# One queue for x and the first weights of a four-branch decoder trunk, with its scheduler's constants fitted anew

## The chip, the cores and the metric

The kernel runs on one core of a Trainium2 chip. Its time is device microseconds of one execution, and the number compared is the median of several runs. TensorE (PE in the profile, PEld for its weight loads) multiplies matrices, VectorE (DVE) and ScalarE (ACT) work on elements, GpSimd (POOL) fills constants and moves a few small tiles, SyncE (SP) issues most loads. ACT and POOL can issue loads too; "SPq", "ACTq" and "POOLq" are the issuing sides of these engines.

## The reference

One layer of a decoder trunk on x of 256 tokens by 1024 channels, float32. A row norm, one projection to 4104 columns, four branches side by side of 256 channels each, a projection back, a second row norm, and the residual:

```python
h = rmsnorm(x, pre_norm_g[l])
proj = jnp.einsum('btd,dc->btc', h, w_in[l])
p_gdn, p_hgrn, p_moba, p_diff = jnp.split(proj, splits, axis=-1)
y = jnp.concatenate([gdn_branch(...), hgrn2_branch(...), moba_branch(...), diff_branch(...)], axis=-1)
y = jnp.einsum('btc,cd->btd', y, w_out[l])
x = x + rmsnorm(y, post_norm_g[l])
```

"gdn" is a gated delta rule in chunks of 64 tokens with a short convolution ahead of it, "hgrn" a gated linear recurrence, "moba" a causal softmax attention (with 256 tokens only one block), "diff" the difference of two softmax attentions. Each has four heads and a SiLU gate.

## The kernel before

**Operands.** Every large product is done in a reduced float32 format (fp32r) as three products of high and low parts: hi·hi + lo·hi + hi·lo. A weight pair (two blocks of 128 rows of one column group, 512 or 520 columns wide) is loaded into a buffer `raw` (six of them), and `split` makes `whi` (a rounding copy, on ACT) and `wlo` (a subtraction, on DVE) from it, four buffers each. x comes transposed (`pxt`, 35 columns of small parameters and then eight blocks of 128 channels by 256 tokens). For each block, `hT_hi` is a scaled copy on ACT, `hT_lo` a subtraction on DVE. The row norm of x is not applied there: it is worked out from `xs`, x in rows, and multiplied in after the projections (`rs`, and `rrow`, its copy along the free axis).

**Column groups.** `w_in` is stored in eight groups: gkq, gv (gdn), hqf, hiz (hgrn), mqk, mvz (moba), dqk, dvz (diff). `piece` loads and splits a pair when a projection first asks for it. gkq comes first and consists of four pairs: row blocks 0 and 1, 2 and 3, 4 and 5, 6 and 7. For each row block, four matmul groups of three products write to two banks of `pj`. The first pair is treated apart: its two blocks are loaded and split one after the other, and block 0 is rounded on DVE. The other pairs are loaded and split whole.

**Loads of the start.** The tile `px` (traced as h_kd, whose memory it shares) takes the 35 parameters and block 0 of x, and the tiles `xr` (traced as prob) the other seven blocks in four loads of 1, 2, 2 and 2 blocks. All five are issued on ACT. The weights and xs are issued on SP.

**Warm-up.** Ahead of the first data TensorE runs `WARM` matmuls on zeros (from the tile zero, traced as g_nb, into bank wA).

**Order.** Nothing in the program is in the order in which it is written. Every operation is recorded with an engine, a modelled cost, what it reads and writes, and a part letter (`c.part`): "x" for the start with gkq and gv, "g" gdn, "h" hgrn, "m" and "M" moba's first projection with its attention and the rest, "d" and "D" the same for diff, "o" the output projection. `plan` then simulates the engines: whenever an engine is free it takes the ready operation of the highest rank, where rank is the modelled length of the path to the end plus a boost and a `LEAD` by part (the lead only where the boost is under `BOOST`, 30000 ns). Splits of weights carry the boost 30000, the loads of the start more than that, in the order of the blocks (`turn`). `emit` writes each engine's instructions in the order found, and the engines run them in that order. Other constants: `LAT` is the modelled latency from the end of an operation to its reader on another engine, `free` the time at which each engine starts, `HOLD` how far a rank must lead for ACT to change its function table, `STAY` the same for a change of TensorE's tile shape. All instructions that `emit` writes have line L392 in the profile (L390: table loads), so the profile is read by tile names.

Of the kernel before, what the change touches and what calls it, by code (L numbers as in the profile page):

```python
# [29 lines left out]
D = 1024  # L30
T = 256
# [52 lines left out]
R_END = 1160  # L84
P_GAIN, P_PRE = 24, 27
P_END = 35
WARM = 18
BOOST = 30000.0
ORDER = "m d M h D"
KTS = "gmdh"  # L90
# [7 lines left out]
class Core:  # L98
# [2 lines left out]

    SETS = {AF.Exp: 6, AF.Ln: 6, AF.Silu: 18}
    OUT = ("out", "accum_out", "dst")
    HOLD = 71859
    SWITCH, KEEP, STAY = 95, 1e9, 10357
    LEAD = {'h': 9467, 'g': 7491, 'o': -78342, 'M': -634, 'x': 25587, 'm': 2702, 'd': 2886, 'D': 6239}
    WINDOW = 4096 / 1.2
    LAT = {"PE": 200, "DVE": 170, "ACT": 170, "POOL": 170, "SP": 1900}

    def __init__(self, ctx, tc):  # L110
        self.tc, self.nc = tc, tc.nc
# [163 lines left out]
    def dma(self, out, in_, eng="SP"):  # L275
        n = 4.0
        for d in out.shape:
            n *= d
        wr = [] if out.tensor.name not in self.known else [out]
        rd = [] if in_.tensor.name not in self.known else [in_]  # L280
        self.record(eng, "dma_start", max(n / 360.0, 475) if eng == "SP" else 475, wr, rd, (out, in_), {})
        if eng != "SP":
            self.ops[-1].lat = 1900 + n / 360.0

    def move(self, out, in_):

# [8 lines left out]
    def plan(self, noise=None):  # L295

        import heapq
        ops = self.ops
        lat = lambda p, o: 0 if p.eng == o.eng and p.eng == "PE" else (90 if p.eng == o.eng and p.fn != "dma_start" else p.lat)
        if not ops[0].succs:  # L300
            for i, o in enumerate(ops):
                o.preds.discard(i)
# [7 lines left out]
            if noise is not None:  # L310
                o.rank += noise[i]
        ready = {e: [] for e in self.engines}
        free = dict(dict.fromkeys(self.engines, 0.0), SP=500.0)
        events = [(0.0, 0, i) for i, o in enumerate(ops) if not o.left]
        due = {}
        heapq.heapify(events)
# [2 lines left out]
        while events:  # L319
            t = events[0][0]  # L320
            while events and events[0][0] <= t:
                _, kind, i = heapq.heappop(events)
                if kind == 0:
                    heapq.heappush(ready[ops[i].eng], (-ops[i].rank, i))
            for e, q in ready.items():
                if not q or free[e] > t:
                    continue
                i = heapq.heappop(q)[1]
                o = ops[i]
                if e == "PE" and mode != o.mode:  # L330

                    more = [x for x in q if ops[x[1]].mode == mode and -x[0] > o.rank - (self.KEEP if mode != (128, 128) else self.STAY)]
                    if more:
                        heapq.heappush(q, (-o.rank, i))
                        x = min(more)
                        q.remove(x)
                        heapq.heapify(q)
                        i = x[1]
                        o = ops[i]
                cost = o.cost  # L340
                if o.need is not None and o.need != cur:

                    same = [x for x in q if ops[x[1]].need in (None, cur) and -x[0] > o.rank - self.HOLD]
                    if same:
                        heapq.heappush(q, (-o.rank, i))
                        x = min(same)
                        q.remove(x)
                        heapq.heapify(q)
                        i = x[1]
                        o = ops[i]  # L350
# [7 lines left out]
                if e == "PE":  # L358
# [6 lines left out]
                    k = int((o.at + 630) / self.WINDOW)  # L365
# [7 lines left out]
                for s in o.succs:  # L373
                    n = ops[s]
# [31 lines left out]
def _build(c, x, pxt, w_in, w_out, cst, prow, out, dbg):  # L406
# [11 lines left out]
    turn = lambda k: BOOST * (4.0 - 0.2 * k)  # L418
    c.boost = turn(0)
    c.dma(px[:, 0:P_END + T], pxt[:, 0:P_END + T], "ACT")  # L420
    XPARTS = [(1, 2), (2, 4), (4, 6), (6, 8)]
    for a, b in XPARTS:
        c.boost = turn(a)
        c.dma(xr[a // 2][:, a % 2:a % 2 + b - a],
              pxt[:, P_END + a * T:P_END + b * T].rearrange("p (k t) -> p k t", t=T), "ACT")
    for j in range(2):
        c.boost = turn(9 + j)
        c.dma(xs[:, j], x[j * 128:(j + 1) * 128, :])
# [7 lines left out]
    BLOCKS, BLOCK_AT, o = {}, {}, 0  # L436
# [3 lines left out]
    RAW, HI, LO = {}, {}, {}  # L440

    def piece(key, k):

        if (key, k) not in HI:
            t = c.tmp("raw", [128, 2, 520], bufs=6)
            first = not HI
            w, o = BLOCKS[key], BLOCK_AT[key] + k * 128 * BLOCKS[key]
            part = bass.AP(tensor=w_in.tensor, offset=w_in.offset + o, ap=[[2 * w, 128], [w, 2], [1, w]])
            lead = sum(1 for q in HI if q[0] != "o")
            c.boost = turn(k) - 0.05 * BOOST if lead < 8 else turn(8) if lead < 10 else 0.0  # L450
            if first:
                c.dma(t[:, 0, :w], part[:, 0])
                c.boost = turn(1) - 0.05 * BOOST
                c.dma(t[:, 1, :w], part[:, 1])
            else:
                c.dma(t[:, :, :w], part)
            split([(key, k), (key, k + 1)], t[:, :, :w], first)
        return HI[key, k], LO[key, k]

    def split(keys, raw, apart=False):  # L460

        w = raw.shape[2]
        c.boost = BOOST
        hi = c.tmp("whi", [128, 2, 520], bufs=4, dt=FR)[:, :, :w]
        lo = c.tmp("wlo", [128, 2, 520], bufs=4, dt=FR)[:, :, :w]
        for i in ([slice(0, 1), slice(1, 2)] if apart else [slice(0, 2)]):
            if apart and i.start == 0:
                c.copy(hi[:, i], raw[:, i])
            else:
                act(hi[:, i], raw[:, i], AF.Copy)  # L470
            c.tt(lo[:, i], raw[:, i], hi[:, i].bitcast(F), OP.subtract)
        for i, key in enumerate(keys):
            HI[key], LO[key] = hi[:, i], lo[:, i]
        c.boost = 0.0
# [18 lines left out]
    warm = c.bank("wA")  # L493
    for _ in range(WARM):
        mm(warm[:, 0:256], zb[:, 0:128], zb)
    for k in range(8):
        c.boost = BOOST + 500.0
        g = px[:, P_PRE + k:P_PRE + k + 1]
        xk = xr[k // 2][:, k % 2] if k else px[:, P_END:P_END + T]
        act(hh_t[:, k], xk, AF.Copy, scale=g)  # L500
        c.stt(hl_t[:, k], xk, g, hh_t[:, k].bitcast(F), OP.mult, OP.subtract)
    c.boost = 0.0
    c.copy(pc, px[:, 0:P_END])
    c.ts(pc[:, P_GAIN + 2:P_GAIN + 3], pc[:, P_GAIN + 2:P_GAIN + 3], 1.0 - lam_init, None, OP.mult)

    rs = c.tile("rs", [128, 2])
# [663 lines left out]
    for i, (name, kt) in enumerate(KT):  # L1170
        t = c.tmp("raw", [128, 2, 520], bufs=6)
# [3 lines left out]
        for j in range(2):  # L1175
            cols = slice(j * 128, (j + 1) * 128)
            for m, (c0, w) in enumerate(PARTS[j]):
                n, o = divmod(c0, 512)
# [63 lines left out]
```

## Time and profile before

| what | value |
|---|---|
| median of 3 runs | 174.97 us (173.48 to 176.22) |
| the profiled execution | 175.41 us, its span 173.7 us |
| mean granted TensorE clock | 0.974 |
| busy: PE, DVE, ACT, POOL | 160.8, 132.9, 106.8, 15.7 us |
| bytes moved | 27.24 MB, mean 157 GB/s |
| first matmul on data, last matmul's end | 5.33 us, 167.95 us |

The page gives busy times by engine, the span in 40 slices of 4.34 us (each digit the busy share in tenths, PEclk the clock granted to TensorE), the chain of work that ended last, and groups of instructions. A stretch of the span, asked for by its bounds, is shown as one row: bounds, length, then for PE, PEld, DVE, ACT and POOL the busy time with the number of instructions that touch the stretch, then the granted clock, the busy share of the DMA engines, and GB/s. A row of the timeline has the start, the duration, the engine, the line, the operation, out<-in, and in brackets how long the engine had stood before it and what ended that. A row of the chain has the start, the duration and what it was. A row on DMA issues ends with the median time from issue to landing in us. A row of waits has who waited, for whom, us in total, times, and the longest.

### The profile page before, as it was taken

Reading aid. Unit: us, or ns where it says so; the run is one execution under the profiler, and the core shown is the slowest. Engines: PE = TensorE matmul, PEld = TensorE weight load, DVE = VectorE, ACT = ScalarE, POOL = GpSimd, SP = SyncE. Lnnn points to the kernel's source line nnn. Section 1 sums busy time; section 2 is a strip of 40 time slices with the busy share of each in tenths; the row PEclk is TensorE's granted clock in tenths of the full one; section 3 lists DMA queues with packets and bytes.
Section 4 is the critical chain, followed back from the end, with each engine's and each line's share of the span. In section 5 each row is a group of like instructions: output and inputs, shape, how many; then the busy total and the mean of one; then the engine's idle time right before and its main releaser. Section 6 shows DMA issues by size and latency. Waiting matters only on the chain.

```text
span 173.7 us, 3605 instructions
## 1 busy us (share of the span) xinstructions
PE 160.8 (93%) x1358; PEld 140.1 (81%) x1358; DVE 132.9 (77%) x354; ACT 106.8 (61%) x211; POOL 15.7 (9%) x35
## 2 busy tenths in 40 slices
PE   7759999999999999699999997999999999999960
PEld 4559999899997999698788994776877768987850
DVE  0777599695798999994656996976889668759472
ACT  2684757999634264424598928898699631366440
POOL 8000000000000000265007500000000000000000
PEclk9858999999999999999999999999999999999997
DMA  5999897266194037335004899457706100000033
GB/s 164 339 415 418 338 367 261 55 202 199 53 312 157 0 116 235 138 76 110 0 4 91 218 296 398 149 180 246 248 0 189 56 0 0 4 0 0 0 121 121
DMA packets 14176, 27.24 MB, mean 157 GB/s; under 512 B 1360, under 2 KB 2640, under 8 KB 14160
## 3 DMA queue, kind: packets, MB, share of 16 engines
q1 hardware_dynamic: 12288, 24.39, 40.8%
q0 software_dynamic: 1152, 1.57, 4.4%
q10 hardware_dynamic: 720, 1.07, 2.0%
q8 instruction: 10, 0.16, 0.4%
q14 instruction: 6, 0.05, 0.1%
HBM read 24.14 MB, written 1.05 MB: 145 GB/s over the span
## 4 chain that ended last, share of the span: by engine, by line
PE 74%; DVE 12%; DMA 7%; ACT 2%; issue 1%; ACTq 1%; DVEq 0%
PE pj L392 49%; PE gA L392 7%; PE gB L392 7%; PE wB L392 6%; PE wA L392 6%; DVE wlo L392 5%; DMA prob<-in_pxt_dram 4%; DMA raw<-in_w_in_dram 3%; DVE g_nb L392 2%; ACT whi L392 1%; DVE g_vb L392 1%; ACTq L392 1%; DVE g_y L392 1%; DVE b4k L392 1%; DVE lf L392 1%
## 5 line engine op out<-in xcount | busy, mean ns | idle before, releaser
L392 DVE TENSOR_TENSOR wlo<-raw,whi 128x1024 fp32r<-128x1024 f32 (+2 forms) x41 | 48.1, 1197 | 11.1 <-ACT whi L392 6.4
L392 ACT ACTIVATE whi<-raw 128x1024 fp32r<-128x1024 f32 (+2 forms) x40 | 41.4, 1047 | 19.1 <-PE pj L392 12.0
L392 PE MATMUL pj<-hT_hi,whi 128*128 128x256 f32 x144 | 38.8, 293 | 4.1 <-ACT whi L392 1.9
L392 PE MATMUL pj<-hT_lo,whi 128*128 128x256 f32 x144 | 38.1, 290 | 0.0
L392 PEld LDWEIGHTS pj<-hT_hi,whi 128*128 128x128 f32 x144 | 28.1, 196 | 6.0 <-ACT whi L392 3.8
L392 PE MATMUL pj<-hT_hi,wlo 128*128 128x256 f32 x144 | 28.9, 292 | 0.2 <-DVE wlo L392 0.2
L392 PEld LDWEIGHTS pj<-hT_lo,whi 128*128 128x128 f32 x144 | 28.1, 197 | 0.1
L392 PE MATMUL pj<-whi,hT_lo 128*128 128x512 f32 (+2 forms) x80 | 26.7, 348 | 0.0
L392 PEld LDWEIGHTS pj<-hT_hi,wlo 128*128 128x128 f32 x144 | 22.2, 194 | 0.9 <-DVE wlo L392 0.6
L392 PE MATMUL pj<-wlo,hT_hi 128*128 128x512 f32 (+2 forms) x64 | 21.3, 348 | 0.7 <-DVE wlo L392 0.7
L392 PE MATMUL pj<-whi,hT_hi 128*128 128x512 f32 (+2 forms) x64 | 21.4, 342 | 0.5 <-DVE gz_moba L392 0.5
L392 PEld LDWEIGHTS pj<-whi,hT_lo 128*128 128x128 f32 x80 | 15.0, 188 | 1.7
L392 PEld LDWEIGHTS pj<-whi,hT_hi 128*128 128x128 f32 x64 | 12.0, 189 | 2.1 <-DVE gz_moba L392 0.9
L390 ACT ACT_TABLE_LOAD x9 | 11.5, 1283 | 3.4 <-issue 3.2
L392 PEld LDWEIGHTS pj<-wlo,hT_hi 128*128 128x128 f32 x64 | 11.6, 188 | 2.3 <-DVE wlo L392 1.1
L392 ACT ACTIVATE prob<-prob,mx 128x128 f32<-128x128 f32 (+1 forms) x24 | 10.7, 448 | 3.4 <-DVE mx L392 3.3
L392 DVE CUSTOM_DVE_ANT_0 prob<-wB,cs 128x128 f32<-128x128 f32 (+1 forms) x24 | 7.8, 356 | 6.4 <-PE wB L392 6.4
L392 POOL DMA_DIRECT2D d_st<-d_ks x12 | 6.1, 506 | 68.2 <-ACT d_ks L392 68.2
L392 PE MATMUL pj<-whi,d_st 128*128 128x512 f32 (+1 forms) x32 | 10.1, 390 | 0.0
L392 POOL DMA_DIRECT2D d_st<-qk4k x12 | 5.9, 492 | 13.5 <-PE wB L392 11.8
L392 PEld LDWEIGHTS pj<-whi,d_st 128*128 128x128 f32 x32 | 5.4, 189 | 1.1 <-DVE d_st L392 0.2
L392 ACT ACTIVATE t2k<-pj 128x512 f32<-128x512 f32 (+1 forms) x4 | 2.2, 544 | 5.3 <-PE pj L392 5.3
(269 smaller groups left out, 287.4 us busy)
## 6 DMA issues: line engine op xcount, KB each, us to landing
raw<-in_w_in_dram SPq DMA_DIRECT2D x27, 512.0 KB, 5.9
raw<-in_w_out_dram SPq DMA_DIRECT2D x8, 512.0 KB, 4.5
raw<-in_w_in_dram SPq DMA_DIRECT2D x4, 520.0 KB, 8.2
xs<-in_x_dram SPq DMA_DIRECT2D x2, 512.0 KB, 8.5
prob<-in_pxt_dram ACTq DMA_DIRECT2D x3, 256.0 KB, 6.8
d_st<-d_ks POOLq DMA_DIRECT2D x12, 64.0 KB, 2.0
d_st<-qk4k POOLq DMA_DIRECT2D x12, 64.0 KB, 2.0
raw<-in_w_in_dram SPq DMA_DIRECT2D x2, 256.0 KB, 3.7
```

What stands on the lines that cost most here:

```text
L390: nc.scalar.add_instruction(mybir.InstLoadActFuncSet(name=nc.get_next_instruction_name(), act_func_set_id=cur, ins=[], outs=[]))
L392: getattr(self.engines[o.eng], o.fn)(*o.args, **o.kw)
```

## The change

The four loads of `xr` move from ACT to SP, between the weights that they go with; only `px` stays on ACT. The first two weight pairs, not the first alone, are loaded and split block by block; only block 0 of the first is rounded on DVE, the other three on ACT. The copy of the small parameters, `pc`, gets a boost below all others. WARM goes from 18 to 19. `LEAD`, `HOLD`, `STAY`, the modelled load latencies, the latency within one engine, and the engines' modelled start times take new values. Nothing else is changed in what is computed.

```diff
-WARM = 18
+WARM = 19
...
-    HOLD = 71859
-    SWITCH, KEEP, STAY = 95, 1e9, 10357
-    LEAD = {'h': 9467, 'g': 7491, 'o': -78342, 'M': -634, 'x': 25587, 'm': 2702, 'd': 2886, 'D': 6239}
+    HOLD = 56014
+    SWITCH, KEEP, STAY = 95, 1e9, 15899
+    LEAD = {'h': 2263, 'g': 1067, 'o': -118175, 'M': -12485, 'x': 58212, 'm': 15360, 'd': 889, 'D': -7580}
...
-    LAT = {"PE": 200, "DVE": 170, "ACT": 170, "POOL": 170, "SP": 1900}
+    LAT = {"PE": 200, "DVE": 170, "ACT": 170, "POOL": 170, "SP": 2600}
...
-            self.ops[-1].lat = 1900 + n / 360.0
+            self.ops[-1].lat = 2600 + n / 360.0
...
-        lat = lambda p, o: 0 if p.eng == o.eng and p.eng == "PE" else (90 if p.eng == o.eng and p.fn != "dma_start" else p.lat)
+        lat = lambda p, o: 0 if p.eng == o.eng and p.eng == "PE" else (120 if p.eng == o.eng and p.fn != "dma_start" else p.lat)
...
-        free = dict(dict.fromkeys(self.engines, 0.0), SP=500.0)
+        free = dict(PE=1150.0, DVE=880.0, ACT=800.0, POOL=0.0, SP=800.0)
...
-    XPARTS = [(1, 2), (2, 4), (4, 6), (6, 8)]
-    for a, b in XPARTS:
+    for a, b in ((1, 2), (2, 4), (4, 6), (6, 8)):
         c.boost = turn(a)
         c.dma(xr[a // 2][:, a % 2:a % 2 + b - a],
-              pxt[:, P_END + a * T:P_END + b * T].rearrange("p (k t) -> p k t", t=T), "ACT")
+              pxt[:, P_END + a * T:P_END + b * T].rearrange("p (k t) -> p k t", t=T))
...
-            first = not HI
...
-            c.boost = turn(k) - 0.05 * BOOST if lead < 8 else turn(8) if lead < 10 else 0.0
+            first = lead < 4
             if first:
-                c.dma(t[:, 0, :w], part[:, 0])
-                c.boost = turn(1) - 0.05 * BOOST
-                c.dma(t[:, 1, :w], part[:, 1])
+                for i in range(2):
+                    c.boost = turn(k + i) - 0.05 * BOOST
+                    c.dma(t[:, i, :w], part[:, i])
             else:
+                c.boost = turn(k) - 0.05 * BOOST if lead < 8 else turn(8) if lead < 10 else 0.0
                 c.dma(t[:, :, :w], part)
-            split([(key, k), (key, k + 1)], t[:, :, :w], first)
+            split([(key, k), (key, k + 1)], t[:, :, :w], first, not lead)
...
-    def split(keys, raw, apart=False):
+    def split(keys, raw, apart=False, first=False):
...
-            if apart and i.start == 0:
+            if first and i.start == 0:
                 c.copy(hi[:, i], raw[:, i])
             else:
                 act(hi[:, i], raw[:, i], AF.Copy)
...
+    c.boost = -BOOST
     c.copy(pc, px[:, 0:P_END])
+    c.boost = 0.0
```

## The prediction, made before the change was run

> **What bounds the kernel now.** I read the page's busy shares and slices first, then the chain, then stretches of the span cut where TensorE's state changes.
>
> ```profile
> span 173.7 us, 3605 instructions
> PE 160.8 (93%) x1358; PEld 140.1 (81%) x1358; DVE 132.9 (77%) x354; ACT 106.8 (61%) x211; POOL 15.7 (9%) x35
> PE   7759999999999999699999997999999999999960
> PEclk9858999999999999999999999999999999999997
> PE 74%; DVE 12%; DMA 7%; ACT 2%; issue 1%; ACTq 1%; DVEq 0%
> ```
>
> TensorE is busy in 93% of the span and holds 74% of the chain. What is not "9" in its row lies in the first three slices (4.34 us each), two places in the middle (slices 16 and 24, counted from 0), and the end. The granted clock falls in slices 1 to 3 (the last slice holds no matmul). So the time is TensorE's work, plus holes, plus work done at a lower clock.
>
> ```profile
> core 0: us, PE busy (x) PEld busy (x) DVE busy (x) ACT busy (x) POOL busy (x), PEclk, DMA share, GB/s
> 5.33:8.68 3.35, 3.13 (x15) 2.30 (x15) 2.31 (x6) 1.95 (x4) 0.00 (x0) 0.86 1.00 348
> 8.68:10.57 1.89, 0.00 (x2) 0.00 (x1) 0.93 (x4) 1.51 (x3) 0.00 (x0) 0.50 1.05 405
> 10.57:14.40 3.83, 3.83 (x18) 3.83 (x19) 3.83 (x5) 3.15 (x5) 0.00 (x0) 0.50 1.04 421
> 14.40:22.09 7.69, 7.69 (x66) 7.69 (x66) 5.00 (x8) 4.66 (x7) 0.00 (x0) 0.99 0.95 371
> ...
> 34.26:70.00 35.74, 35.35 (x314) 33.92 (x314) 31.35 (x83) 21.99 (x34) 0.00 (x0) 1.00 0.51 164
> 70.00:75.00 5.00, 3.56 (x31) 3.38 (x30) 4.91 (x32) 2.28 (x3) 1.64 (x3) 1.00 0.36 113
> 75.00:105.00 30.00, 30.00 (x370) 26.48 (x369) 22.28 (x73) 18.18 (x55) 10.17 (x21) 1.00 0.48 120
> 105.00:110.00 5.00, 3.78 (x16) 2.27 (x15) 4.07 (x10) 4.91 (x7) 0.00 (x0) 1.00 1.01 375
> 110.00:167.95 57.95, 57.89 (x426) 46.19 (x424) 44.56 (x103) 35.76 (x74) 0.00 (x0) 1.00 0.25 81
> ```
>
> The first projection, block "gkq", takes 96 matmuls (8 row blocks of x, 4 column groups, 3 products) from 5.33 to 22.09 us, 16.8 us. In the fourth row it runs at 7.69/66 = 0.117 us each, in the third at 3.83/18 = 0.213 us with the clock at 0.50. All 96 at the first pace are 11.2 us. What is lost: 15 in 3.35 us, 1.6 us over pace; 1.89 us with nothing; 18 at half clock, 1.7 us over. Together **5.2 us**. From 34 to 168 us only 0.39, 1.44, 1.22 and 0.06 us are idle, 3.1 in all.
>
> Why the front stalls is told by the chain and the first microseconds:
>
> ```profile
> 2.21 6.83 DMA prob<-in_pxt_dram
> 9.06 0.51 ACT hT_hi L392
> 9.57 0.96 ACT whi L392
> ...
> 10.57 12.05 PE pj L392 x84
> ```
>
> ```profile
> 0.80 0.40 ACTq L392 DMA_DIRECT2D h_kd<-in_pxt_dram  x1
> 0.80 5.56 SPq L392 DMA_DIRECT2D raw<-in_w_in_dram  x6
> 1.23 1.96 ACTq L392 DMA_DIRECT2D prob<-in_pxt_dram  x4
> 3.22 1.28 ACT L390 ACT_TABLE_LOAD   x1 [3.22 <-issue]
> 4.48 0.18 DVE L392 COPY pc<-h_kd 128x35 f32<-128x35 f32 x1 [3.38 <-DMA h_kd<-in_pxt_dram]
> 4.77 0.42 DVE L392 CAST whi<-raw 128x512 fp32r<-128x512 f32 x1
> 5.10 0.48 DVE L392 SCALAR_TENSOR_TENSOR hT_lo<-h_kd,hT_hi 128x256 fp32r<-128x256 f32 x1
> 5.50 0.69 DVE L392 TENSOR_TENSOR wlo<-raw,whi 128x512 fp32r<-128x512 f32 x1
> 5.83 0.61 ACT L392 ACTIVATE whi<-raw 128x512 fp32r<-128x512 f32 x1
> 9.47 1.04 ACT L392 ACTIVATE whi<-raw 128x1024 fp32r<-128x1024 f32 x1
> 10.55 1.23 DVE L392 TENSOR_TENSOR wlo<-raw,whi 128x1024 fp32r<-128x1024 f32 x1 [0.46 <-ACT whi L392]
> ```
>
> ScalarE waits to 9.06 us for a part of x (tile prob), and the weights of row blocks 2 and 3 are split behind it, 9.47 to 10.51; TensorE restarts at 10.57. Yet it had done 15 of the 24 matmuls that blocks 0 and 1 allow: nine, 1.1 us of work, stood behind one that needed blocks 2 and 3. The order expected these earlier than they came.
>
> **The change part by part.** *One queue.* Two queues filled the transfer engines at once, so the late parts of x took bytes from the weights needed first. The bytes that move:
>
> ```profile
> 0.00:5.00 5.00, 3.36 (x15) 2.04 (x15) 0.72 (x6) 1.76 (x2) 3.94 (x11) 1.00 0.60 179
> 5.00:10.00 5.00, 3.13 (x15) 2.33 (x15) 3.46 (x8) 2.91 (x7) 0.00 (x0) 0.78 1.01 364
> 10.00:15.00 5.00, 4.43 (x22) 4.43 (x23) 4.54 (x7) 3.79 (x7) 0.00 (x0) 0.54 1.04 419
> d_st<-d_ks POOLq DMA_DIRECT2D x12, 64.0 KB, 2.0
> h_kd<-in_pxt_dram ACTq DMA_DIRECT2D x1, 145.5 KB, 3.7
> SPq L392 <- DMA h_kd<-in_pxt_dram: 2.1, 1, 2.1
> ```
>
> That is 0.90 MB by 5 us, 2.7 by 10 and 4.8 by 15; the last 419 GB/s is SP's queue alone, so one queue fills the engines. In the new order the sums are 0.41 MB to weights 0, 0.80 to weights 1, 1.33 to weights 2, 1.59 to weights 3, 2.38 to weights 4 and 5, 3.16 to weights 6 and 7. At the rates above these have moved at about 3.6, 4.7, 6.2, 6.9, 9.1 and 11.1 us. Landing comes up to 0.9 us later (estimate: h_kd landed at 0.80 + 3.7 = 4.5, and a 64 KB copy takes 2.0 in all). Weights 2 are then split by ScalarE by 6.8 to 7.7 us instead of 10.51.
>
> TensorE's need at 0.117 us is 1.4 us for each row block. From 5.0 us it wants block 2 at 7.8, blocks 4 and 5 at 10.6, blocks 6 and 7 at 13.4. They are ready (1.04 us after landing) at about 7.7, 11.0 and 13.0. So one small wait, up to 0.5 us, stays at block 4. DVE asks 0.69 + 0.48 = 1.17 us a block, less than 1.4, but at block 0 also the 0.42 cast, which keeps some 0.3 us of the start's unevenness. I book 0.7 of the 1.6 us again.
>
> SP issues ten loads for gkq where it issued five, ACT one where it issued five. Six issues in 5.56 us include the wait of 2.1 us for h_kd; the four on ACT show 0.49 us each. Ten at 0.49 end near 5.7 us, or 7.8 with such a wait, and the last, weights 6 and 7, is wanted on the wire after 2.64 MB, at 9.8 us. Behind them stand the gv weights and xs, which by their boosts come after gkq's in both kernels: nothing. If issue took twice as long it would be 10.6 us and cost about 0.8.
>
> *ACT's own queue* loses 1.96 us of issues, so the table load ends near 2.5 instead of 4.50 us, and hT_hi of block 0 waits for h_kd alone. With the move of pc's copy (boost lowered; its first reader is the convolution, which needs the whole of gkq) DVE can cast the weights at 4.48 instead of 4.77. First matmul 5.0 instead of 5.33: 0.3 us, bounds 0 (h_kd lands no sooner) and 0.8.
>
> *Splitting the second pair:* one more DMA, one more ScalarE copy, one more DVE subtraction: 2 x 0.61 - 1.04 = 0.2 us of ACT, 2 x 0.69 - 1.23 = 0.15 of DVE, under TensorE's work. Two 256 KB loads may also run at the 364 GB/s of the mixed row rather than at 419: 0.52 MB, 0.2 us. The Trainium skill ("DMA: Bandwidth & Descriptors", Bandwidth) speaks against the split: it advises batches of at least 1 MiB. No run here shows a lone small load from HBM; with others in flight, the sum by that rule loses no more than the 0.2 us just named.
>
> *One warm matmul more* (128x256, so 0.2 us at the half-clock pace) runs before the first data, or fills a gap: nothing.
>
> *The scheduler's constants* add no instruction but reorder all queues after the front. The stated latencies rise (1.9 to 2.6 us for loads), which mends just the fault of the nine matmuls. Their effect past 22 us isn't in the trace. Bounds: the 3.1 us of middle holes go (-3.1), or holes grow by up to what the front gives (+4.8) and, in the case below, more. I take 0, the nearest row being 30 us at a stretch without a hole.
>
> Sum: 0.3 + 1.9 + 1.7 + (1.6 - 0.7) = **4.8 us**. The profiled execution took 175.41 us (span 173.7 and 1.7 around it), so 170.6; the median of the runs shown, 174.97, is 0.44 lower, so **170.2**. A difference under 2% (171.5 to 178.5) is about what this kernel's measurement can't tell from none.
>
> **The rivals.**
>
> 1. *The clock falls again.* The clock fell near 7.7 us (0.86 over the stretch to 8.68 puts 0.94 us of it at half), with some eleven of the 15 matmuls run since 5.33 and only 0.22 us of that stretch idle. If the new front is as thin before 7.7, some 3.4 us run at 0.213: up to 1.7 us back, 171.9. For: block 0 still waits for DVE. Against: from 5.0 us there should be some 18 matmuls by then (2.7 us less 0.7, by 0.117). Chance 0.17. The Trainium skill ("TensorE: Matmul & The Clock Gate", Part 1) names an idle window of some 3.4 us as the cause of half rate; by that there would be no fall in either kernel, so the trace disagrees, and the row decides.
>
> 2. *The middle takes it back.* DVE's order carries both the splits of weights and the delta-rule's 15 serial steps:
>
> ```profile
> PE pj L392 <- DVE g_nb L392: 1.4, 1, 1.4
> 14.93 1.06 ACT L392 ACTIVATE b4k<-xs 128x1024 f32<-128x1024 f32 x1 [1.10 <-DMA xs<-in_x_dram]
> 23.14 0.37 ACT L392 ACTIVATE rrow<-gA 128x256 f32<-128x256 f32 x1
> L392 DVE STREAM_SHUFFLE g_nb<-g_d x15: 289/298/312, 60.1 to 75.8; 128x128 f32<-128x128 f32 x15
> ```
>
> TensorE waited 1.4 us there. xs, from which the row norm comes, still lands near 15 us, behind the same bytes; if the delta-rule keeps its time while TensorE arrives 5 us sooner, that wait grows by 2 to 5 us: 172.5 to 175.5, middle 174. For: the serial steps bind DVE at 4.91 of 5 us. Against: the row norm (rrow) was only made at 23.14 us, some 6 us after its inputs, so 3 us of it can come forward. Chance 0.15.
>
> 3. *Slower: the attention ahead of the delta rule.* The lead of part "m" against "g" rises from -4.8 to +14.3 us. If its DVE work stands before the serial steps, and projections' subtractions behind these, TensorE starves for the steps' length instead of 1.4 us: between 4.5 us (15 shuffles of 0.30 alone) and 15.7 (60.1 to 75.8, with what stands between them), say 10. Then 170.2 + 10 = 180. It decides when projection work is used up before the steps end, which the trace missed by 1.4 us. Against: weight splits carry a boost of 30 us and get past the steps. Chance 0.06.
>
> 4. *The new order also closes the holes.* 3.1 us less, 167.1; chance 0.15.
>
> 5. *The queue doesn't do what it says* (issue pace, or landing much later): the front keeps most of its stall; within 1.5 us of before, 174. Chance 0.05, told apart from 2 by the front alone.
>
> **How the numbers follow.** My forecast, gain 4 to 6 us: chance 0.42, 169 to 171.4; the rivals as given. Faster by over 2%: 0.42 + 0.15 and a third of rival 1, about 0.63. Slower: 0.06. The rest, 0.31. The range takes rival 4 at its lower end and rival 2 to past its middle: 166.8 to 174.8.
>
> **What would show it.** In the changed profile: the gkq matmuls without a hole near 9 us and done by about 17 us instead of 22.09; the clock at 1.00 through 15 us; ACT's table load ending before 3 us; x loads on SP's row; after that TensorE's row full, with its last matmul near 163 us instead of 167.95. The forecast is wrong if gkq ends after 19 us, or if idle stretches past 34 us sum to much more than 3 us.

## The result, and the profile after

The changed kernel took 169.55 us, the median of four runs (169.09 to 169.74). The kernel before took 175.08 us beside it (173.48 to 176.22). The ratio is 0.971, with a 95% interval of 0.964 to 0.978. The forecast was 170.2 us, a gain of 4.8; measured was a gain of 5.5. The profiled execution took 169.37 us. The size came out nearly right, but the parts of the sum did not. Four executions, two of run 2 and two of run 4 below (one of these of 385 us), fell into a slower state: the medians contain them, the ratios do not.

The changed kernel's page, busy shares and slices:

```profile
span 167.5 us, 3631 instructions
PE 158.0 (94%) x1359; PEld 138.1 (82%) x1359; DVE 131.6 (79%) x355; ACT 106.0 (63%) x212; POOL 15.7 (9%) x35
...
PE   7899999999999999989999999999989999999960
...
PEclk9999999999999999999999999999999999999996
```

The 6 and the 7 in the middle of TensorE's row are gone, and the granted clock shows no fall. TensorE's busy time fell as well, from 160.8 to 158.0 us with one matmul more; some of that is the half clock of the first profile, since a second profile of the kernel before (below) has 159.0. Stretches of the changed kernel, cut at the first matmul on data, at its wait at 8.21, at the end of gkq, and then as before:

```profile
4.98:8.21 3.23, 2.72 (x16) 2.03 (x16) 2.56 (x6) 2.08 (x5) 0.00 (x0) 1.00 1.02 346
8.21:17.89 9.68, 9.68 (x81) 9.68 (x82) 8.11 (x13) 7.26 (x13) 0.00 (x0) 1.00 1.03 411
...
34.26:70.00 35.74, 35.38 (x298) 32.59 (x298) 33.60 (x126) 23.43 (x50) 2.10 (x4) 1.00 0.54 169
70.00:100.00 30.00, 29.44 (x361) 26.81 (x360) 23.18 (x65) 15.67 (x38) 9.70 (x20) 1.00 0.47 129
100.00:130.00 30.00, 29.56 (x205) 22.32 (x204) 24.89 (x65) 27.89 (x55) 0.00 (x0) 1.00 0.60 178
130.00:140.00 10.00, 9.54 (x80) 7.71 (x80) 9.04 (x26) 4.39 (x9) 0.00 (x0) 1.00 0.09 33
140.00:161.80 21.80, 21.79 (x174) 18.45 (x173) 12.55 (x20) 9.25 (x20) 0.00 (x0) 1.00 0.06 21
```

The block gkq runs from 4.98 to 17.89 instead of 5.33 to 22.09 us. Its hole is gone: 81 matmuls follow each other in 9.68 us. Behind 34 us TensorE is idle for 0.36 + 0.56 + 0.44 + 0.46 + 0.01 = 1.83 us, before 3.1. The last matmul ends at 161.8 instead of 167.95. So 4.2 us were gained by the end of gkq, and 2.0 more behind it.

The changed kernel's first microseconds, from the timeline:

```profile
1.24 1.28 ACT L390 ACT_TABLE_LOAD   x1 [1.24 <-PEq L1233]
...
2.18 0.43 SPq L392 DMA_DIRECT2D raw<-in_w_in_dram  x1
2.65 0.43 SPq L392 DMA_DIRECT2D prob<-in_pxt_dram  x1
...
3.61 0.95 POOL L392 MEMSET ath<- 128x1024 f32 x1
...
4.04 0.79 DVE L392 CAST whi<-raw 128x512 fp32r<-128x512 f32 x1 [2.94 <-DMA raw<-in_w_in_dram]
...
4.98 0.47 PE L392 MATMUL pj<-hT_hi,whi 128*128 128x256 f32 x2 [0.33 <-DVE pc L392]
...
7.03 0.63 ACT L392 ACTIVATE whi<-raw 128x512 fp32r<-128x512 f32 x1 [1.15 <-DMA raw<-in_w_in_dram]
7.65 0.91 ACT L392 ACTIVATE hT_hi<-prob,h_kd 128x256 fp32r<-128x256 f32 x2
...
8.21 0.51 PE L392 MATMUL pj<-hT_hi,whi 128*128 128x256 f32 x2 [0.34 <-ACT hT_hi L392]
```

The rows at 2.18 and 2.65 issue the weights of row block 2 and then x of blocks 2 and 3; they land at 7.00 and 7.62. ScalarE now splits these weights at 7.03, as soon as they have landed, and this x behind them. DVE's first cast starts earlier than before (4.04, not 4.77), but takes 0.79 us instead of 0.42.

### The profile page after: what moved, and what is told of

It reads as the page before. It is cut to its first block, busy times and chain, and to the rows that moved or that the text cites. A ratio compares the mean times of both kernels' runs of the same rounds, so it can differ in the third digit from the quotient of the medians.

```text
span 167.5 us, 3631 instructions
## 1 busy us (share of the span) xinstructions
PE 158.0 (94%) x1359; PEld 138.1 (82%) x1359; DVE 131.6 (79%) x355; ACT 106.0 (63%) x212; POOL 15.7 (9%) x35
## 4 chain that ended last, share of the span: by engine, by line
PE 72%; DVE 17%; issue 3%; DMA 3%; ACT 2%; SPq 1%; DVEq 0%; ACTq 0%
PE pj L392 51%; PE gA L392 7%; PE gB L392 6%; PE wA L392 5%; PE wB L392 3%; DVE g_nb L392 3%; DMA raw<-in_w_in_dram 3%; DVE wlo L392 2%; DVE prob L392 1%; DVE y L392 1%; DVE g_y L392 1%; DVE g_kdec L392 1%; DVE g_vb L392 1%; ACT t2k L392 1%; DVE g_d L392 1%
## 5 line engine op out<-in xcount | busy, mean ns | idle before, releaser
L392 ACT ACTIVATE whi<-raw 128x1024 fp32r<-128x1024 f32 (+2 forms) x41 | 40.8, 1024 | 14.3 <-PE pj L392 8.1
L392 PE MATMUL pj<-hT_hi,whi 128*128 128x256 f32 x144 | 37.3, 289 | 1.2 <-DVE qk4k L392 0.6
L392 PE MATMUL pj<-hT_lo,whi 128*128 128x256 f32 x144 | 35.9, 284 | 0.0
L392 PEld LDWEIGHTS pj<-hT_hi,whi 128*128 128x128 f32 x144 | 26.3, 188 | 2.8 <-ACT hT_hi L392 1.2
L392 PEld LDWEIGHTS pj<-hT_lo,whi 128*128 128x128 f32 x144 | 26.2, 189 | 0.1
L392 PEld LDWEIGHTS pj<-hT_hi,wlo 128*128 128x128 f32 x144 | 21.7, 188 | 0.7 <-DVE wlo L392 0.6
L392 PE MATMUL pj<-wlo,hT_hi 128*128 128x512 f32 (+2 forms) x64 | 19.0, 342 | 0.0
L392 PEld LDWEIGHTS pj<-wlo,hT_hi 128*128 128x128 f32 x64 | 11.1, 188 | 1.1
L392 PE MATMUL pj<-whi,d_st 128*128 128x512 f32 (+1 forms) x32 | 9.3, 374 | 0.0
```

What stands on the lines that cost most here:

```text
L392: getattr(self.engines[o.eng], o.fn)(*o.args, **o.kw)
```

## The experiments

Time is compared as a ratio to the kernel before, run on the same chip. In the summary, "gkq" is the time at which that block ends in the profile, "rest" the time from there to the end of the last matmul.

| run | median us | ratio (95%) | gkq | rest |
|---|---|---|---|---|
| before, first profile | 175.41 (that execution) | | 22.09 | 145.9 |
| before, second profile | 173.61 (that execution) | | 19.93 | 146.2 |
| changed | 169.55 | 0.971 (0.964, 0.978) | 17.89 | 143.9 |
| 1: x back on ACT | 171.04 | 0.981 (0.977, 0.985) | 20.00 | 143.8 |
| 2: before, x on SP | 174.54 | 0.998 (0.994, 1.002) | 19.96 | 145.6 |
| 3: second pair whole | 169.35 | 0.972 (0.967, 0.976) | 17.96 | 143.9 |
| 4: old leads | 173.43 | 0.995 (0.991, 0.999) | 17.98 | 147.6 |
| 5: new constants alone | 177.86 | 1.020 (1.012, 1.029) | 21.02 | 151.1 |
| 6: 15 warm matmuls fewer | 170.00 | 0.973 (0.966, 0.981) | 18.70 | 143.9 |
| 7: old lead of m | 187.97 | 1.076 (1.068, 1.084) | 18.03 | 162.5 |
| 8: before, nine matmuls first | 173.20 | 0.993 (0.990, 0.995) | 19.73 | 145.8 |
| 9: old latencies | 170.16 | 0.977 (0.972, 0.982) | 18.41 | 144.1 |
| 10: front mended | 170.63 | 0.980 (0.975, 0.984) | 18.90 | 143.9 |
| 11: old leads but m's | 172.65 | 0.993 (0.990, 0.997) | 18.07 | 147.4 |

**The kernel before, profiled a second time**, with no edit.

> The kernel before once more, unchanged, for a second profile, since the first one fell on a run with the mean clock at 0.974 where most runs have 0.993. If the clock's fall at 7.7 us is a matter of chance, this profile has gkq's end near 20.4 instead of 22.09 us, the clock at 1.00 through 15 us, and a time of 173.2 to 174.7. If the fall belongs to the kernel, the profile repeats the first one.

Its page, and its stretches:

```profile
PE   7769999999999999699999997999999999999960
...
PEclk9999999999999999999999999999999999999996
```

```profile
8.44:10.03 1.59, 0.00 (x1) 0.01 (x1) 0.51 (x2) 1.45 (x3) 0.00 (x0) 1.00 1.04 395
10.03:19.93 9.90, 9.90 (x82) 9.78 (x82) 8.71 (x12) 7.82 (x12) 0.00 (x0) 1.00 1.03 394
...
140.00:166.10 26.10, 26.10 (x220) 21.90 (x218) 18.64 (x41) 11.56 (x25) 0.00 (x0) 1.00 0.05 17
```

Its ScalarE at the hole, and the load of the weights of blocks 2 and 3, issued at 1.71 us:

```profile
8.27 0.51 ACT L392 ACTIVATE hT_hi<-prob,h_kd 128x256 fp32r<-128x256 f32 x1 [0.51 <-DMA prob<-in_pxt_dram]
8.92 1.06 ACT L392 ACTIVATE whi<-raw 128x1024 fp32r<-128x1024 f32 x1
```

```profile
raw<-in_w_in_dram SPq DMA_DIRECT2D x1, 512.0 KB, 7.2
```

The hole in gkq is here too, 1.59 us, but the granted clock shows no fall, and gkq ends at 19.93 instead of 22.09 us. The weights of blocks 2 and 3 land at 1.71 + 7.2 = 8.9 us and are split at once (9.2 and 9.47 in the first profile). Of the 56 executions of the kernel before that ran beside runs 1 to 11, 15 had a mean granted clock under 0.98, with a median of 174.86 us, and 35 one of 0.99 or more, with 174.0. So a fall as large as in the prediction's profile (0.974) is not in most executions, and those with one are some 0.9 us longer. Against this second profile the front gains 2.0 us (19.93 to 17.89), not 4.2, and the part behind it 2.3 (146.2 to 143.9).

**1. x back on ACT, all orders else as in the changed kernel**

```diff
+        xl = [i for i in order if self.ops[i].fn == "dma_start" and self.ops[i].args[1].tensor.name == "in_pxt_dram"]
+        for i in xl:
+            self.ops[i].eng = "ACT"
+        at = order.index(xl[0])
+        order = order[:at] + xl + [i for i in order[at:] if i not in xl]
```

> The changed kernel with every engine's order of work kept; only the four loads of x go back to ACT's queue, issued right behind h_kd. Queue theory (late parts of x take bytes from the weights needed first, and ACT's issues delay its table load): weights 2 land near 8.5 us instead of 7.0, the table load ends near 4.5, gkq's last matmul moves from 17.8 to 20 us or later, and the time rises by 2 to 3 us, to about 172. Order theory (the queues don't matter, the scheduler's new latencies do): gkq ends within 0.7 us of 17.8 and the time stays at 169.5 to 170.3.

Of its ScalarE timeline:

```profile
4.92 1.28 ACT L395 ACT_TABLE_LOAD   x1 [4.92 <-DMA h_kd<-in_pxt_dram]
6.21 0.51 ACT L397 ACTIVATE hT_hi<-h_kd 128x256 fp32r<-128x256 f32 x1
...
7.55 0.61 ACT L397 ACTIVATE whi<-raw 128x512 fp32r<-128x512 f32 x1
```

gkq ends 2.1 us later (20.00), and the time is 1.7 us above that of run 3, which ran beside it. But the loss is not near 9 us: weights 2 are split at 7.55, ahead of x of blocks 2 and 3, and no hole follows. It is at the start, where the first split of x comes at 6.21 instead of 4.21 us. Some of that comes from the way this run is built: the table load came to stand behind the wait for the first load, 1.28 us that the kernel before doesn't pay there. The granted clock of this profile is also at 0.50 from 7.65 to 11.06 us, as in two of the run's four executions by their means, which are 0.2 us longer than the other two. So 1.7 us is more than the queue itself is worth with this order.

**2. The kernel before, with x on SP between the weights**

```diff
...
+        order = [i for i in order if i not in xl[1:]]
+        for i, w in zip(xl[1:], (ws[0], ws[1], ws[2], ws[3])):
+            self.ops[i].eng = "SP"
+            order.insert(order.index(w) + 1, i)
...
```

> The kernel before with every engine's order of work kept; only the loads of x go to SP's queue, each behind the weights that stood ahead of it. Queue theory: weights 2 and 3 land near 7.8 us instead of 9.4, the hole before 10.57 us shrinks to under 0.7 us, the clock stays up or is back sooner, gkq ends by 19.5 instead of 22.0, the time falls by 2.5 us or more. Order theory: nine matmuls still stand behind blocks 2 and 3, the hole stays over 1 us, gkq ends after 21, the time falls by less than 1 us.

Of its ScalarE timeline, and its load of the weights of blocks 2 and 3, issued at 2.65 us:

```profile
8.65 0.51 ACT L400 ACTIVATE hT_hi<-prob,h_kd 128x256 fp32r<-128x256 f32 x1 [1.64 <-DMA prob<-in_pxt_dram]
9.06 1.04 ACT L400 ACTIVATE whi<-raw 128x1024 fp32r<-128x1024 f32 x1
```

```profile
raw<-in_w_in_dram SPq DMA_DIRECT2D x1, 512.0 KB, 5.3
```

The queue alone changed nothing in the time: 0.998, gkq at 19.96. Yet it did bring the weights forward: those of blocks 2 and 3 land at 2.65 + 5.3 = 8.0 us, where the two profiles of the kernel before have 9.2 and 8.9. ScalarE doesn't use this: it had split x of blocks 0 to 3 and then stood 1.64 us for x of block 4, with the weights of blocks 2 and 3 behind that in its order. TensorE restarts at 10.15. So ScalarE's order is a second hold on the restart, beside the landing; what the new order does without the earlier landing is seen in run 5.

**3. The second pair loaded and split whole**

```diff
-            first = lead < 4
+            first = lead < 2
```

> The changed kernel with the second weight pair loaded and split whole. If the split is worth what its landing suggests, block 2's first matmul starts near 9.0 instead of 8.21 us and gkq ends 0.5 to 0.8 us later, the time is about 170.1. If VectorE's pace sets the front, gkq ends within 0.2 us of 17.8 and the time is the same, 169.5.

169.35 against 169.55 us, gkq 17.96 against 17.89: the split of the second pair is worth nothing that these runs can tell, in either direction. The first matmul of block 2 does come later, at 9.27 instead of 8.21 us, but by then TensorE has done more of blocks 0 and 1.

**4. The changed kernel with LEAD, HOLD and STAY of before**

```diff
-    HOLD = 56014
-    SWITCH, KEEP, STAY = 95, 1e9, 15899
-    LEAD = {'h': 2263, 'g': 1067, 'o': -118175, 'M': -12485, 'x': 58212, 'm': 15360, 'd': 889, 'D': -7580}
+    HOLD = 71859
+    SWITCH, KEEP, STAY = 95, 1e9, 10357
+    LEAD = {'h': 9467, 'g': 7491, 'o': -78342, 'M': -634, 'x': 25587, 'm': 2702, 'd': 2886, 'D': 6239}
```

> The changed kernel with LEAD, HOLD and STAY of the kernel before; its loads and its front are the same as after the change. If the part of the gain behind gkq (6.15 us at the last matmul less 4.2 at gkq's end, some 1.9 us) comes from the leads, gkq still ends near 17.8 but the holes behind 34 us grow from 1.8 to 3 us or more, and the time is 171 to 171.8. If the leads are only noise around the same total, the time is 169 to 170.2.

173.43 us: with the front kept (gkq 17.98) and the old leads, 1.1 of the 5 us are left (0.2 to 1.5 by the interval). On the same chip run 3 took 169.35, so the leads are worth 4.1 us here. Its last stretch:

```profile
140.00:165.60 25.60, 24.84 (x204) 20.35 (x203) 18.20 (x40) 10.43 (x23) 0.00 (x0) 1.00 0.05 18
```

Its waits, and where it does the last two gates (tile y), then the same two rows of the changed kernel:

```profile
PE pj L392 <- DVE g_nb L392: 1.4, 1, 1.4
```

```profile
L392 DVE TENSOR_TENSOR y<-y,gz_diff x1: 669/669/669, 146.7 to 146.7; 128x512 f32<-128x512 f32 x1
L392 DVE TENSOR_TENSOR y<-y,gz_hgrn x1: 691/691/691, 152.1 to 152.1; 128x512 f32<-128x512 f32 x1
```

```profile
L392 DVE TENSOR_TENSOR y<-y,gz_diff x1: 691/691/691, 139.8 to 139.8; 128x512 f32<-128x512 f32 x1
L392 DVE TENSOR_TENSOR y<-y,gz_hgrn x1: 693/693/693, 144.3 to 144.3; 128x512 f32<-128x512 f32 x1
```

With the old leads the wait for g_nb is there (1.4 us), and diff and hgrn are gated at 146.7 and 152.1, so that TensorE goes to the end with 0.76 us of holes. With the new ones they are gated 7 to 8 us earlier and the last 21.80 us of matmuls run without one. Of the 3.8 us between the ends of the last matmuls (165.6 and 161.8), idle time behind 34 us accounts for 1.4 (1.42 + 0.40 + 0.68 + 0.76 = 3.26 against 1.83). The remaining 2.4 us stand in the records as busy time: 160.5 against 158.0 us for the same 1359 matmuls. Some of it can be found: matmuls that use only a part of TensorE's rows or columns run side by side where the order puts them next to each other. The 16 matmuls from m_pt and kf, in run 4 and then in the changed kernel (rows for TensorE alone):

```profile
143.36:145.17 1.81, 1.81 (x16) 1.00 0.00 0
```

```profile
135.92:137.08 1.16, 1.16 (x16) 1.00 0.00 0
```

In the changed kernel they start in pairs, one into bank gA and one into gB, and take 0.65 us less. The eight into gB from b4k and cs stand in one group instead of two (0.6 us less), and the 56 from sall and m_pt differ by 0.3. That is some 1.6 of the 2.4 us; the rest was not isolated.

**5. The kernel before with all new constants, loads and splits as they were.** WARM, LEAD, HOLD, STAY, the latencies and `free` take the new values of the diff above.

> The kernel before with all the new scheduler constants (LEAD, HOLD, STAY, latencies, start times, WARM) and nothing else: x on ACT's queue, second pair whole, pc's copy where it was. If constants and loads add up (E4 and E1: constants some 3.5 to 4 us, loads and front 1 to 1.5), the time is 170.5 to 171.5, with gkq's end near 20 us. If the leads help only on the front for which they were fitted, it is 173 or more.

177.86 us, slower than before by 1.2 to 2.9%. Its split of the weights of blocks 2 and 3, two later stretches (the second for TensorE alone), and the clock row of its page:

```profile
8.85 1.06 ACT L392 ACTIVATE whi<-raw 128x1024 fp32r<-128x1024 f32 x1 [0.72 <-DMA raw<-in_w_in_dram]
```

```profile
126.00:134.00 8.00, 6.58 (x36) 5.44 (x34) 7.91 (x16) 7.94 (x10) 0.00 (x0) 1.00 0.18 64
```

```profile
136.48:143.31 6.83, 6.83 (x32) 0.50 0.00 1
```

```profile
PEclk9999999999999999999999999999998589999995
```

At the front, ScalarE's new order waits for nothing but the landing, and still TensorE restarts only at 9.96 us: the landing at 8.8 alone holds it there. So the restart near 10 us had two holds, and each was enough: the landing of the weights (old loads, 9.96 here) and ScalarE's order (old order, 10.15 in run 2). With both gone it comes at 9.27 (run 3) or 8.21 (changed). That gkq ends only at 21.02 here has another cause as well: in this profile the matmuls run at half pace up to 13.60 us.

The new constants gain nothing by themselves: on the old loads and splits their order leaves the rest of the kernel at 151.1 us, 5 longer than with the constants of before. From 126 to 134 us TensorE stands for 1.4 of 8 us, and from 136.48 on it runs 6.83 us at half clock, which is up to 3.4 of these 5; the mean clock is 0.97 to 0.98 in all four executions. With run 4 this makes a square: old loads and old leads 174.5, new loads alone 173.43, new constants alone 177.86, both 169.35 to 169.55. It is not quite clean: run 4 keeps the new latencies, which run 9 puts at half a microsecond. The two parts don't add up; the new leads are a gain only with the new loads.

**6. The changed kernel with 15 of the first 16 warm matmuls left out**

```diff
+        zero = [i for i in order if self.ops[i].eng == "PE" and self.ops[i].fn == "matmul" and self.ops[i].kw["rhs"].dtype == BF]
+        order = [i for i in order if i not in zero[1:16]]
```

> The changed kernel with the 15 warm-up matmuls behind the first left out of TensorE's order, all else in the same order. If the warm-up gives the full clock at 5 us, the front now starts at half clock until a busy stretch of 3.4 us has passed (to 8.4 or 11.8 us): 16 matmuls by 8.21 become fewer, gkq ends 1 to 2 us later and the time is 170.6 to 171.5. If the front waits for data and VectorE anyway, gkq ends within 0.5 us of 17.8 and the time is under 170.2.

Its TensorE after the first matmuls:

```profile
6.00:8.50 2.50, 2.50 (x13) 1.00 1.02 352
```

170.00 us, and gkq 0.8 us later, 18.70. The first matmul stands at 4.98 as before, but 13 take 2.50 us, 0.19 each, where 0.117 is the full pace. The slow pace lasts to 9.84 us. The warm matmuls as a whole are worth about this 0.8 us at the front and, by the ratios, some 0.4 us of the time, which is not clear of the noise; what the one added matmul does was not run by itself.

**7. The changed kernel with part m again 4.8 us behind part g**

```diff
-    LEAD = {... 'm': 15360, ...}
+    LEAD = {... 'm': -3722, ...}
```

> The changed kernel with one constant put back: the lead of part m against part g as it was before (-4.8 us instead of +14.3). The front is the same. If putting the first attention ahead of the delta rule is what the leads bring, the time rises to 172 or more, with the holes of 3 us back. If it is harmful, as the prediction's third rival had it, the time falls below 169. If it doesn't matter, 169 to 170.

Its longest wait, and the clock row of its page:

```profile
PE pj L392 <- DVE g_nb L392: 11.2, 1, 11.2
```

```profile
PEclk9999999999999965599999999999999999999999
```

187.97 us, the largest effect of all, 18.4 above the changed kernel. TensorE stands 11.2 us for the delta rule's steps, and the clock falls in slices 14 to 16 in its wake; the rest are smaller waits and the half clock. This is the mechanism of rival 3 with the sign turned round: it is moba's work *behind* the steps, and not ahead of them, that leaves TensorE with nothing to multiply.

**8. The kernel before, with the nine matmuls of blocks 0 and 1 ahead of the first of blocks 2 and 3**

```diff
...
+        last = max(order.index(i) for i in gk if gk[i] < 2)
+        late = [i for i in order[:last] if gk.get(i, 0) >= 2]
+        order = [i for i in order[:last + 1] if i not in late] + late + order[last + 1:]
...
```

> The kernel before, with one edit: in TensorE's order the matmuls of gkq that belong to row blocks 0 and 1 all stand ahead of the first one of blocks 2 and 3 (nine move). Loads, splits and every other engine's order stay. Theory A (the prediction's: nine matmuls, 1.1 us of work, stood behind one that could not start, so part of the hole was a fault of the order): the nine fill the hole of 1.6 to 1.9 us, gkq ends about 1 us earlier than in the second profile of the kernel before (18.9 instead of 19.9 us). If what the front gains passed to the end in full, the time would be 173.5; by the other runs with the old leads (173.43 with the new front, 2 us earlier at gkq's end) only about half passes: 174.0. Theory B (the order did not matter: what waits is the splits of blocks 2 and 3, and the work behind them is only shifted): gkq ends at 19.8 or later, and the time is within 0.3 us of 174.6.

Its TensorE, cut where the pace changes and at the first matmul of blocks 2 and 3:

```profile
5.42:8.98 3.56, 3.56 (x15) 1.00 1.03 369
8.98:10.23 1.25, 1.25 (x10) 1.00 1.04 398
10.23:19.73 9.50, 9.38 (x74) 1.00 1.00 401
```

The nine fill the hole, as meant, yet gkq ends only 0.2 us earlier (19.73 against 19.93): theory B for the front. Blocks 2 and 3 still start when their weights are split (10.23), and the remaining 74 matmuls take 0.128 us each where the second profile of before takes 9.90/82 = 0.121: without the nine between, TensorE now meets short stops (its weight loads wait 0.7 us in all for DVE's subtractions). That the first 15 run at half pace here doesn't bear on this: all 24 of blocks 0 and 1 are done before 10.23. The time is 173.20 us against 174.53, more than the 0.2 us explain; the two profiled executions differ by 0.5 (173.07 and 173.61). What the remainder is stays open.

**9. The changed kernel with the latencies and start times of before**

```diff
-    LAT = {"PE": 200, "DVE": 170, "ACT": 170, "POOL": 170, "SP": 2600}
+    LAT = {"PE": 200, "DVE": 170, "ACT": 170, "POOL": 170, "SP": 1900}
...
-        free = dict(PE=1150.0, DVE=880.0, ACT=800.0, POOL=0.0, SP=800.0)
+        free = dict(dict.fromkeys(self.engines, 0.0), SP=500.0)
```

(and 2600 and 120 to 1900 and 90 in the two other places)

> The changed kernel with the planner's latencies and start times of before (1900 for a load, 90 between instructions of one engine, no start times but SP's), and the new leads, loads and split. Theory A (the prediction's: the higher load latency is what mends the order of the nine matmuls): the plan again puts matmuls of blocks 2 and 3 among those of block 1, TensorE gets a hole of 0.5 to 1 us in gkq, which ends at 18.5 to 19 us instead of 17.9. Theory B (with the loads in order of need the latency does not matter at the front): gkq ends within 0.2 us of 17.9. Behind the front the whole plan is made anew; if leads are worth what they are only together with the latencies they were fitted to, the time is 172 or more; if the leads carry the gain by themselves, it is 169.3 to 171.

170.16 us, gkq 18.41: the latencies are worth about half a microsecond, all of it ahead of gkq's end, and the leads carry their gain without them. No hole near 9 us comes back, so it was not the stated latency that closed it; and with the new latencies too, in the changed kernel, the first matmul of block 2 still stands ahead of eight of blocks 0 and 1. On theory A's own number the run falls between the two (18.41, where A said 18.5 to 19 and B 17.7 to 18.1).

**10. The changed kernel with two moves at the front:** the zeroing of ath from GpSimd to DVE, ahead of the first cast, and on ScalarE x of block 2 ahead of weights 2.

```diff
...
+        ops[ath].eng = "DVE"
+        order.remove(ath)
+        order.insert(order.index(cast), ath)
...
+            order.remove(h)
+            order.insert(order.index(w), h)
...
```

> The changed kernel with two moves at the front: the zeroing of tile ath (0.95 us on GpSimd, to 4.56) is done by DVE ahead of its first cast, where DVE is idle; and on ScalarE the first split of x of block 2 stands ahead of the copy of weights 2 instead of behind it. Theory A (DVE's cast of weights 0 takes 0.79 instead of 0.42 us because GpSimd's zeroing runs beside it; and x of block 2 waits in ScalarE's queue for weights 2, which land at 7.03): the cast takes 0.42 and ends near 4.5 instead of 4.83, the first matmul is at about 4.7 instead of 4.98, TensorE does not wait at 8.21, gkq ends at 17.2 to 17.6 instead of 17.89, and the time falls by 0.3 to 0.6 to about 169.0. Theory B (the cast ends at 4.83 for another reason, the landing of its load): the cast still ends at 4.8, gkq ends within 0.2 of 17.9, and the time is within 0.2 us of 169.5.

Its first microseconds:

```profile
4.07 0.43 DVE L406 CAST whi<-raw 128x512 fp32r<-128x512 f32 x1 [1.89 <-DMA raw<-in_w_in_dram]
...
4.82 0.50 PE L406 MATMUL pj<-hT_hi,whi 128*128 128x256 f32 x2 [0.28 <-ACT hT_hi L406]
...
7.62 0.51 ACT L406 ACTIVATE hT_hi<-prob,h_kd 128x256 fp32r<-128x256 f32 x1 [1.33 <-DMA prob<-in_pxt_dram]
8.04 0.61 ACT L406 ACTIVATE whi<-raw 128x512 fp32r<-128x512 f32 x1
...
8.70 0.50 PE L406 MATMUL pj<-hT_hi,whi 128*128 128x256 f32 x2 [0.98 <-ACT whi L406]
```

One half holds: without GpSimd's zeroing beside it the cast takes 0.43 us and ends at 4.50, and the first matmul starts at 4.82. The other half falls. x of block 2 lands only at 7.60 us, since its load is issued behind that of weights 2 (2.65 and 2.18 us), which land at 6.98. So in the changed kernel it did not wait in ScalarE's queue, as theory A had it, and put first it holds the weights up to 8.04: TensorE stands 0.98 us, gkq ends 1.0 us later, and so does the kernel (170.63).

**11. The kernel of run 4 with m's lead raised alone**

```diff
-    LEAD = {... 'm': 2702, ...}
+    LEAD = {... 'm': 21784, ...}
```

> The new loads, splits and latencies with the leads, HOLD and STAY of before (the kernel of 173.43 us), but with the lead of part m raised from 2702 to 21784, so that m stands 14.3 us ahead of g as in the changed kernel. What is open is which of the leads brings the 3.9 us. Theory A (m alone: with moba's first projection and its attention ahead of the delta rule's steps, the wait of 1.4 us for g_nb goes and the later parts come forward together): the wait goes, and the time is 169.5 to 171. Theory B (the leads work only as a set, since the end is gained by diff and hgrn being done 8 to 10 us earlier, and their leads are left as they were): the wait for g_nb may go, y_diff and y_hgrn stay near 147 and 152 us, and the time is 172.5 or more, or slower than before if the projections run out elsewhere.

Two of its waits:

```profile
PE pj L392 <- DVE g_nb L392: 1.3, 1, 1.3
PE pj L392 <- ACT y_gdn L392: 1.2, 1, 1.2
```

172.65 us, and its rest is 147.4 as in run 4. The wait for g_nb stays, and the late gates come only 1.1 us earlier (145.6 and 151.0). m's lead is needed (run 7) but doesn't bring the gain; the leads work as a set. Which smaller set would do was not run.

## Why the prediction came out right, and which steps did not

**The bound** was read rightly: TensorE's work, plus holes, plus work at half clock. The sum then said: front 4.8 us, leads 0. On the chip the new front with the old leads was worth 1.1 us (run 4), and the leads on top of it 4.1. That the total came within 0.7 us of the forecast is luck.

**The hole of 1.9 us** went, as said. The reason given, that late parts of x took bytes from the weights needed first, is half of it: with x between them the weights of blocks 2 and 3 land 0.9 to 1.2 us earlier (run 2), and without that the new order doesn't help (run 5). The other half was not seen: ScalarE's old order put x of block 4 ahead of these weights, and with it the earlier landing is lost. The higher latencies don't mend the hole (run 9), and moving the nine matmuls alone brings 0.2 us (run 8).

**The half clock, 1.7 us**, was mis-sized. It is in the profiled execution and not in the second one. Executions of before with such a fall are some 0.9 us longer, and they are about a third (21 of 56 with a mean clock under 0.99), so that the median holds little of it; yet the sum took off 1.7 and moved the result by only the 0.44 us between that execution and the median. The row was read rightly; the fault was to take what one execution showed for a property of the kernel. In its profile the changed kernel runs at full pace from the first matmul on data through 15 us, as predicted; rival 1 did not come there.

**The thin start**: 0.7 of 1.6 us was to stay, and 16 matmuls in 3.23 us are 3.23 - 16 x 0.117 = 1.4 us over pace. It hardly improved: the cast took 0.79 us, and weights 2 and x of block 2 landed only at 7.00 and 7.62.

**The first matmul** was to be at 5.0 and is at 4.98, the table load was to end near 2.5 and ends at 2.52, weights 2 were to be split by 6.8 to 7.7 and are by 7.66. These hold, the first and the last in part by chance: the first loads landed up to 0.3 us earlier than before and the cast took 0.4 longer; and the working put x of blocks 2 and 3 ahead of weights 2, with 1.33 MB up to these, where the kernel issues it behind them, so that only 1.07 MB had to come. gkq was to end by about 17 and ended at 17.89.

**The front passes to the end in full**: this holds under the new leads and not under the old. In runs 1, 6, 9 and 10 gkq ends 0.5 to 2.1 us later than in the changed kernel, and the rest stays between 143.8 and 144.1. Under the old leads the second profile of before and run 4 differ by 1.95 us at gkq's end and by 0.5 at the last matmul (166.1 and 165.6): 1.5 us of the front are lost on the way. That is rival 2, the middle takes it back, but not by its mechanism, since the wait for g_nb stays at 1.4 us: idle time behind 34 us is the same (3.2 and 3.3 us), and TensorE's busy time is 1.5 us longer in run 4.

**The leads, taken as 0**, are the step that failed most. The bounds were -3.1 and +4.8, and the choice of 0 rested on a stretch without a hole. Measured is -4.1 us (runs 3 and 4), beyond the lower bound, since the bound counted only idle time, and more than half of the gain lies in time booked as busy, much of it narrow matmuls that now run side by side (run 4). With the old loads and splits all the new constants together are a loss of 3 us (run 5): the term had no value of its own apart from the front. So rival 4, the new order closes holes, came in part (3.1 to 1.83 us of idle time, the wait for g_nb gone), and the forecast of 170.2 stood because a front that gave less met an order that gave more.

**The small terms**: splitting the second pair was to cost 0.2 and costs nothing that can be told (run 3). The warm matmuls, "nothing" for one more, are not without worth as a whole (run 6).

**Rival 3** had its mechanism and price right, about 10 us for starving through the steps (11.2 in run 7), and its direction wrong: with the other new leads, the higher lead of m is what keeps TensorE fed.

## What to carry to other kernels

Look at the granted clock and at more than one execution before a stall at half clock is put into a sum: what one execution shows may be chance, and the median may hold little of it. Where a planner's order changes with its constants, don't book that at nothing because nothing is added: test front and order apart (old order with the new front, new order with the old), since here the new leads were worth 4.1 us with the new loads, and all the new constants together a loss of 3 without them (177.86 against 174.86 beside it). A hole behind a late load can have two holds, the landing and the order of the engine that reads it; ask what stands ahead of the load's reader before the transfers are rearranged, since here neither mend alone moved the restart.

## What the runs showed of the hardware

- **A cast on VectorE waits for GpSimd's zeroing.** In the changed kernel the cast from 4.04 ended at 4.83, 0.27 us after GpSimd's memset (3.61 + 0.95 = 4.56); with the memset elsewhere it took 0.43 us (run 10). In all eight profiles in which the cast starts during this memset, from 4.04 to 4.38 us, it ends at 4.83 or 4.84. The Trainium skill ("SBUF — State Buffer", Who interferes with whom) says that a cast in a two-port mode and a GpSimd instruction share one pair of ports under an exclusive lock, and that whichever comes second blocks. The trace agrees that it blocks, though it ended sooner than a whole cast after the memset (4.56 + 0.42 = 4.98); which mode this cast runs in no run shows.
- **Half pace where the granted clock reads 1.00.** In run 8, 15 matmuls take 3.56 us, and in run 6, 13 take 2.50, with the row of the granted clock at 1.00. The trace's records of the clock begin only at 9.08 and 9.84 us in these runs, just where the pace goes from 0.21 to 0.12 us a matmul, and the row gives 1.00 where there is no record. In run 6 the warm matmuls had been left out, in run 8 not; in run 5, with 16 of them up to 4.75 us, the slow pace lasts to 13.60. In the other profiles, all with warm matmuls, the records begin between 3.80 and 6.34. So the pace at a kernel's start must be read from the matmuls themselves, and warm matmuls don't always buy the full one.
- **Loads on SP's queue landed in the order of their issue.** In all 14 profiles no load issued on SP (56 to 61 in each) landed before one issued ahead of it there. The order of issue, not only the bytes, decided what was there first: in the changed kernel weights 2, issued at 2.18, landed at 7.00, and x of blocks 2 and 3, of the same 256 KB and issued at 2.65, at 7.62.
- **Narrow matmuls run side by side when they are neighbours.** 16 matmuls of 64 rows took 1.16 us in alternation between two banks and 1.81 us largely one bank after the other (run 4).
